# Hybrid decoder block on one core: half of the retention gates made by seven-product multiplication with the queries and keys, and 29 modulation rows summed in the values stage

## The chip, the core and the metric

The kernel runs on one core of a Trainium2 chip. TensorE (PE) multiplies, VectorE (DVE), ScalarE (ACT) and GpSimd (POOL) work element by element, SyncE (SP) issues most DMAs, and 16 DMA engines carry the data. The metric is the device time of one execution in microseconds (us). All numbers are float32; a matmul operand is split into a high part (rounded to the format `fp32r`) and a low remainder, and a product of two split operands is three matmuls: low x high, high x low, high x high.

## The reference, cut to what matters

A decoder block for 1024 tokens of width 1024: a conditioning vector gives six modulation vectors (shift, scale and gate, twice), a token mixer runs retention and dilated attention side by side, an MLP follows.

```python
mod = jax.nn.silu(c) @ w_ada[l] + b_ada[l]
sh1, sc1, g1, sh2, sc2, g2 = jnp.split(mod, 6, axis=-1)
h = modulate(rms_norm(x, norm1_g[l]), sh1, sc1)
proj = h @ w_in                       # rq, rk, rv, rg, attention's q, k, v, two gates
ro = retention(rq, rk, heads(rv))     # 4 heads, chunks of 128 tokens, a running state
ro = group_norm(ro)                   # per token and head, 512 values
ret_out = (jax.nn.silu(rg) * ro) @ w_ret_out
```

`rg` is 2048 wide: 512 columns for each of four heads, which the kernel treats as four blocks of 128 columns a head. `g1`, `sh2`, `sc2` and `g2`, 32 rows of 128 values together, are not needed until retention and attention are done.

## The kernel before, in words

**Layout.** `hh` and `hl` are the high and low part of the modulated input, transposed, eight tiles of 128 channels by 1024 tokens. Everything that multiplies `h` reads them.

**Order of the work.** `Steps` runs step after step; each engine executes its instructions in the order in which the code issues them. The stages that matter here come one after the other.

1. *Queries and keys* (`queries_keys`, line 1216 on, class `Blocks`). Products with weights are taken in pairs of 128 columns. A pair is a 2 x 2 block product done by seven block products (`ORDER`) in place of eight. Each of the seven is four steps of three matmuls of 512 columns. DVE and ACT make the weight sums and splits (`prep`), and take the results apart (`post`, `a_out`). `PAIRS` lists 20 pairs: eight with rotary, six queries and two keys of attention, four pairs of merge gates, which pass through Sigmoid and go to DRAM.
2. *Values* (`values`, line 1339). Ten block products (`VSEQ`), five for each pair of heads, each of four sub-steps of 12 matmuls, one for each 128 tokens. During sub-step `p` of product `i`, ACT and DVE finish the results of the sub-step before (`v_post`) and split the weights of product `i + 1` (`v_w` on ACT, `v_low` on DVE); at the head of a product SP reads the weights of product `i + 2` (`v_load`). Results of products 3, 4 (`i` = 2, 3) go through tiles `vo` of the pool `wraw` (tag `raw`, three buffers) to DRAM; those of products 8 and 9 take tiles of another pool, and those of 5 and 10 the tile that holds their sum. Some buffers of that pool serve as staging for every streamed weight.
3. *Chunks* (`chunk`, line 692). 4 heads x 8 chunks. A chunk updates the state (`kv` products, `state`, split to `stateh`/`statel`), makes the scores of the next chunk (`s_kt`: products `sT`, then `sm`, `smh`, `sml`, and the scaled keys `kh`, `kl`), its output `o`, the normalisation (`bn`, `ba`, `gr`, `onm`) and the transposes of the chunk before (`on_T`). Between these products PE works at a gate block: 4 of the 8 steps of a block in each chunk, six matmuls a step, in two portions. In the first four chunks of a head, `u_final` multiplies the head before by its gates (`on`, `srg`) and writes it out (`y`).
4. Attention, the output projections and the MLP follow; the change does not touch them.

**What sets the order around the change.** In a chunk step, `ahead(2)` prepares the loads of the next step: gate weights (ACT copy, DVE subtract, `split_w`) and modulation rows (`mod_prep`: one DVE multiply with the sum along the row, `accum_out`, and one small add). The step list gives a gate block to every second chunk and one of 32 modulation rows to nearly every chunk. Raw tiles come from `wraw`; the weights' halves from `whl` (three buffers each). PSUM has four single banks for `kv`, `sT`, `kT`, `o` and `oT` in turn and two double banks for gate blocks. A tile takes a buffer of its pool that no earlier tile still needs, and waits until there is one.

Of the kernel before, what the change touches and what calls it, by code (L numbers as in the profile page):

```python
# [17 lines left out]
P = 128  # L18
# [122 lines left out]
def block_kernel(ctx, tc, io, stop=None, dbg=None):  # L141
# [478 lines left out]
    def chunk_tiles():  # L620

        p = R["p"]
        R["j"] = p.tile([P, 2, 4, C], F32R, tag="j", bufs=2, name="j2")
        R["sm"] = p.tile([P, C], F32, tag="sm", bufs=1, name="sm00")
        for n in ("smh", "sml"):
            R[n] = p.tile([P, C], F32R, tag=n, bufs=2, name=n + "00")
        for n in ("kh", "kl"):
            R[n] = p.tile([P, 2, P], F32R, tag=n, bufs=1, name=n + "00")

    def s_kt(i):  # L630
# [49 lines left out]
    def u_final(h, es=range(4), queue=nc.sync):  # L680
        for e in es:
# [8 lines left out]
            queue.dma_start(y_d[h][:, 2 * (i % 2):2 * (i % 2) + 2, e // 2], t.rearrange("p (t x) -> p t x", t=2))  # L690

    def chunk(h, c, ahead, w=None):
        p = R["p"]
        g = NC * h + c
        if g + 3 < NG:
            fetch(g + 3)
        if c % 2 == 0:
            hd["rgw"] = w
            hd["rgp"] = ps_mm(f"rg{h}{c}")

        ks = {0: (5, 6, 6), 1: (6, 7, 8)}.get(g) or [4 * (c % 2) + i for i in (0, 2, 4)]
        if g == 0:
            proj_mm(hd["rgp"], hd["rgw"], range(2))
            s_kt(0)
            proj_mm(hd["rgp"], hd["rgw"], range(2, 5))
        vh, vl = hd["v", g][:, 0], hd["v", g][:, 1]
# [8 lines left out]
        if g == 0:  # L715
            s_kt(1)
        proj_mm(hd["rgp"], hd["rgw"], range(*ks[:2]))
        for i, kv in enumerate(kvs):
# [27 lines left out]
        if g > 0:  # L746
            on_T(*divmod(g - 1, NC))
        proj_mm(hd["rgp"], hd["rgw"], range(*ks[1:]))
        bn = p.tile([P, 6], F32, tag="bn", bufs=2, name=f"bn{h}{c}")
# [9 lines left out]
        hd["o", h, c] = on  # L759
        if c % 2 == 1:  # L760
            hd["srg", h, c // 2] = etile(f"srg{h}{c // 2}")
            nc.scalar.activation(hd["srg", h, c // 2], flat(hd["rgp"]), AF.Silu)
        if h > 0 and c < 4:
# [7 lines left out]
    aq_d = {(p, g, a): dram.tile([P, S], F32, name=f"aqd{p}{g}{a}") for p in range(2) for g in range(3) for a in range(2)}  # L771
    ak_d = {(p, a): dram.tile([P, S], F32, name=f"akd{p}{a}") for p in range(2) for a in range(2)}
    h12_d = [dram.tile([P, 2, 512], F32, name=f"h12d{m}") for m in range(4)]
    xn, wa = [], []
# [362 lines left out]
    k_pairs = [("k", 2, p) for p in range(2)]  # L1137
    PAIRS = [{"r": r_pairs, "a": a_pairs, "g": g_pairs, "k": k_pairs}[i].pop(0) for i in "rargrarkrargrarkgaga"]
    NA = len(PAIRS)
    OA = {}  # L1140

    def a_load(q, part):
        pair = PAIRS[q]
        src = io[{"g": "w_gate2", "a": "w_aq", "k": "w_ak2"}.get(pair[0]) or f"w_r{pair[1]}"]
# [22 lines left out]
    def a_out(q, n, x, y=None):  # L1167
# [9 lines left out]
        elif pair[0] in "ak" and pair[1] == 2:  # L1177
            o = OA[q][i].rearrange("p (r i) -> p r i", r=8)[:, :, 64 * t:64 * t + 64]
            view = lambda z: z.rearrange("p (i r) -> p r i", r=8)
        f = AF.Sigmoid if pair[0] == "g" else AF.Copy  # L1180
        if y is None:
            nc.scalar.activation(o, view(x), f)
        else:
            (nc.vector.tensor_add if n == "12" else nc.vector.tensor_sub)(o, view(x), view(y))
            if pair[0] == "g":
                nc.scalar.activation(o, o, f)
        if n in ("12", "21"):
            if pair[0] == "g":
                dst = gate_d[GATES[2 * pair[1] + i]]
            elif pair[0] == "a":  # L1190
                dst = aq_d[pair[2], pair[1], i]
            elif pair[0] == "k":
                dst = ak_d[pair[2], i]
            else:
                return
# [137 lines left out]
    def v_base_load(hp):  # L1333

        for j in range(2):
            V["m", hp, j] = t = x4(f"vm{hp}{j}")
            nc.sync.dma_start(t.rearrange("p (a b) -> p a b", a=2), m11_d[hp][:, 2 * j:2 * j + 2])

    def values(ahead):
        last = len(VSEQ) - 1  # L1340
        for i, (hp, n) in enumerate(VSEQ):
            if i + 2 <= last:
                v_load(i + 2)
            for p in range(4):
# [14 lines left out]
                if p == 2 and i < last:  # L1359
                    v_low(i + 1, 1)  # L1360

                if i == last - 2 and p == 2:
                    fetch(0)
# [13 lines left out]
        for g in (1, 2):  # L1377
# [9 lines left out]

    later_mods = [G1 + k for k in range(NK)] + [SH2 + k for k in range(NK)] + \
                 [SC2 + k for k in range(NK)] + [G2 + k for k in range(NK)]
# [1432 lines left out]
def pack(x, c, w_ada, b_ada, norm1_g, w_in, rel_bias, ret_gn_g, ret_gn_b,  # L2822
# [16 lines left out]
        "w_rv": _vblocks(w[:, 2048:4096]),  # L2839
        "w_rg": _cols(w[:, 4096:6144]),  # L2840
        "w_aq": _pairs(att[:, :, 0].reshape(1024, 1536)),
# [32 lines left out]
```

## Time and profile before

| | |
|---|---|
| median of three runs | 2176.75 us (2176.67 to 2182.43) |
| the profiled execution | 2179.79 us, span 2178.0 us, granted clock 0.997 |
| PE | 99% of the span, 10060 matmuls |
| DVE / ACT / POOL | 69% / 43% / 8% |
| HBM | 322.03 MB read, 158.23 MB written, 221 GB/s over the span |

In the profile, a row of a timeline holds the start, the time occupied, the engine, the line in kernel.py, the operation, the tiles written and read with their shape, and in brackets the idle time before it and what ended it. "L1285 DVE ... vwl<-vwl,vwh" is line 1285 on VectorE, which writes `vwl` from `vwl` and `vwh`. A row of a table of stretches has, for a stretch of the span, each engine's busy time and number of instructions. A row of waits names who waited, for whom, the sum, how often, and the longest. A row of DMA issues ends with the median time from issue to landing.

### The profile page before, as it was taken

How to read it: one execution, taken by the hardware profiler on the slowest of the kernel's cores; microseconds unless marked ns; L12 is line 12 of the kernel's file. 1: busy time of each engine (PE TensorE's matmuls, PEld its weight loads, DVE VectorE, ACT ScalarE, POOL GpSimd, SP SyncE). 2: the span in 40 equal slices, each digit the busy share in tenths (PEclk: the TensorE clock that was granted, in tenths of full speed). 3: DMA queues.
4: the chain of work that ended last, by engine and by line, in shares of the span. 5: the costliest groups of instructions: out<-in, count | busy, mean ns of one | idle time of the engine just before them, and what ended most of it. 6: DMA issues, size and time to landing. Idle time of an engine off the chain costs nothing. (4 is left out here: it accounts for less than half of the span.)

```text
span 2178.0 us, 27354 instructions
## 1 busy us (share of the span) xinstructions
PE 2151.7 (99%) x10060; PEld 1789.6 (82%) x10060; DVE 1512.8 (69%) x2361; ACT 947.4 (43%) x1741; POOL 167.2 (8%) x199
## 2 busy tenths in 40 slices
PE   8999999999999999999999999999999999999998
PEld 6888888888887888888888888888778888888887
DVE  5885777776346787785657644777876665877855
ACT  5553322323343354455657625434454445533413
POOL 0001111100002121211110000001000000000003
PEclk9999999999999999999999999999999999999999
DMA  9759998833568455546777275653244435645322
GB/s 383 282 212 311 270 334 255 235 110 116 184 240 295 160 203 182 173 168 196 205 192 209 98 260 196 222 188 136 66 179 153 153 136 195 248 138 174 109 87 78
DMA packets 161522, 420.98 MB, mean 193 GB/s; under 512 B 27877, under 2 KB 55788, under 8 KB 158316
## 3 DMA queue, kind: packets, MB, share of 16 engines
q1 hardware_dynamic: 149112, 370.70, 47.7%
q0 software_dynamic: 9584, 48.24, 9.8%
q8 instruction: 79, 1.29, 0.2%
q10 hardware_dynamic: 2692, 0.30, 0.1%
q14 instruction: 55, 0.45, 0.1%
HBM read 322.03 MB, written 158.23 MB: 221 GB/s over the span
## 5 line engine op out<-in xcount | busy, mean ns | idle before, releaser
L207 PE MATMUL qap<-hh,qaw 128*128 128x512 f32 x240 | 93.4, 389 | 0.0
L209 PE MATMUL qap<-hl,qaw 128*128 128x512 f32 x240 | 93.4, 389 | 0.0
L211 PE MATMUL qap<-hh,qaw 128*128 128x512 f32 x240 | 93.4, 389 | 0.0
L617 POOL TENSOR_TENSOR j<-qk,j 128x512 fp32r<-128x512 f32 x32 | 43.2, 1351 | 457.5 <-ACT j L616 457.5
L2193 POOL TENSOR_TENSOR accnf<-accnf,sqnf 128x256 f32<-128x256 f32 (+1 forms) x18 | 16.6, 921 | 609.6 <-ACT sqnf L2189 609.6
L2297 ACT ACTIVATE a<-a 128x512 f32<-128x512 f32 x48 | 30.3, 631 | 73.3 <-DVE a L2296 73.3
L2505 ACT CAST w2h<-w2s 128x512 fp32r<-128x512 f32 x36 | 22.4, 621 | 78.7 <-DVE w2s L2543 71.8
L264 DVE TENSOR_TENSOR fw<-w1r,fw 128x512 fp32r<-128x512 f32 x48 | 32.9, 688 | 33.5 <-ACT fw L254 33.5
L209 PEld LDWEIGHTS qap<-hl,qaw 128*128 128x128 f32 x240 | 45.0, 188 | 9.4
L211 PEld LDWEIGHTS qap<-hh,qaw 128*128 128x128 f32 x240 | 45.0, 188 | 9.3
L207 PEld LDWEIGHTS qap<-hh,qaw 128*128 128x128 f32 x240 | 45.0, 188 | 9.3
L652 ACT COPY sm<-sT 128x128 f32<-128x128 f32 x32 | 8.5, 265 | 98.9 <-PE sT L640 91.4
L2028 DVE TENSOR_TENSOR rwl<-rwl,rwh 128x1024 fp32r<-128x1024 f32 x25 | 30.2, 1221 | 29.0 <-ACT rwh L2058 29.0
L207 PE MATMUL fp<-h2h,fw 128*128 128x512 f32 x128 | 50.0, 391 | 0.0
L211 PE MATMUL fp<-h2h,fw 128*128 128x512 f32 x128 | 49.8, 389 | 0.0
L209 PE MATMUL fp<-h2l,fw 128*128 128x512 f32 x128 | 49.8, 389 | 0.0
L207 PE MATMUL roa<-rh,rwl 128*128 128x512 f32 x128 | 49.8, 389 | 0.0
L209 PE MATMUL roa<-rl,rwh 128*128 128x512 f32 x128 | 49.8, 389 | 0.0
L211 PE MATMUL roa<-rh,rwh 128*128 128x512 f32 x128 | 49.8, 389 | 0.0
L1561 ACT ACTIVATE P<-P,ng 128x128 f32<-128x128 f32 (+1 forms) x96 | 41.9, 438 | 17.5 <-DVE ng L1553 17.5
L264 DVE TENSOR_TENSOR qaw<-wa,qaw 128x512 fp32r<-128x512 f32 x60 | 40.0, 686 | 8.8 <-ACT qaw L254 8.8
L292 DVE TENSOR_TENSOR qat<-qat,qap 128x512 f32<-128x512 f32 x20 | 13.7, 687 | 46.4 <-PE qap L211 46.4
(3094 smaller groups left out, 7241.4 us busy)
## 6 DMA issues: line engine op xcount, KB each, us to landing
v<-vd SPq DMA_DIRECT2D x32, 512.0 KB, 4.3
raw<-in_w_ada_dram SPq DMA_DIRECT2D x32, 512.0 KB, 5.0
w1r<-in_w_ff_dram SPq DMA_DIRECT2D x32, 512.0 KB, 4.6
yt<-y POOLq DMA_DIRECT2D x24, 512.0 KB, 7.4
xsd<-as SPq DMA_DIRECT2D x24, 512.0 KB, 2.9
w2r<-in_w_ff2s_dram SPq DMA_DIRECT2D x24, 512.0 KB, 6.7
em<-in_w_ada_dram SPq DMA_DIRECT2D x16, 512.0 KB, 10.2
wrvs<-in_w_rv_dram POOLq DMA_DIRECT2D x16, 512.0 KB, 9.6
```

Of the source, the lines that this page charges most:

```text
L207: nc.tensor.matmul(o, wl, xh, start=first, stop=False, skip_group_check=skip)
L209: nc.tensor.matmul(o, wh, xl, start=False, stop=False, skip_group_check=skip)
L211: nc.tensor.matmul(o, wh, xh, start=False, stop=last, skip_group_check=skip)
L264: nc.vector.tensor_sub(t[:, 512:], src, fv(t[:, :512]))
L292: nc.vector.tensor_sub(u, u, b)
L617: nc.gpsimd.tensor_sub(t[:, 1], src, fv(t[:, 0]))
L652: nc.scalar.copy(sm, ps[:, :C])
L1561: nc.scalar.activation(v, v, AF.Exp, bias=ng[:, blk:blk + 1], accum_out=st[:, g, blk, 2 + a:3 + a])
L2028: nc.vector.tensor_sub(lo, fv(lo), fv(hi))
L2193: (nc.vector if f == 7 else nc.gpsimd).tensor_add(G["acc", key], G["acc", key], sq)
L2297: nc.scalar.activation(o, o, AF.Relu)
L2505: nc.scalar.copy(hi, src)
```

## The change

1. The 16 gate blocks are parted: of each head, blocks 0 and 1 stay in the chunks; blocks 2 and 3 become a pair of the queries-and-keys stage (`"s"`, after all other pairs), pass through Silu there and go to DRAM (`srg_d`). The fifth and the seventh chunk of a head read them back. The weights are rearranged on the host's side accordingly.
2. In the chunks, a table `RG` says how many gate steps each does: 6 in the first of all, then 2, and 1 in the last chunk of a head (64 in all). A block may start in the middle of a head; `rg_mm` takes the next weights and PSUM tile when one is done, `rg_out` applies Silu.
3. 29 of the 32 later modulation rows are read and summed in the values stage, at places listed in `MODS`: six each in products 1 and 2, five each in 5, 6 and 7, two in 8. A call loads row `i` and sums row `i - 2`. The three left stay in the chunks, one in the fifth of each head but the first.
4. `chunk_tiles` allocates the tile `j` last and not first.

```diff
+    RG = [[2] * (NC - 1) + [1] for _ in range(H)]
+    RG[0][0] = 6
+    def rg_mm(n):
+        for _ in range(n):
+            if hd.get("rgk", NK) == NK:
+                hd["rgk"], hd["rgw"], hd["rgp"] = 0, hd["rgws"].pop(0), ps_mm("rg")
+            proj_mm(hd["rgp"], hd["rgw"], [hd["rgk"]])
+            hd["rgk"] += 1
+            if hd["rgk"] == NK:
+                hd["rgs"] = hd["rgp"]
+    def rg_out(h, c):
+        if "rgs" in hd:
+            i = hd["rgi"] = hd.get("rgi", -1) + 1
+            t = hd["srg", i // 2, i % 2] = etile(f"srg{i // 2}{i % 2}")
+            nc.scalar.activation(t, flat(hd.pop("rgs")), AF.Silu)
+        if c in (4, 6):
+            e = c // 2
+            hd["srg", h, e] = etile(f"srg{h}{e}")
+            nc.sync.dma_start(hd["srg", h, e], srg_d[h, e - 2])
...
     def chunk(h, c, ahead, w=None):
...
-        proj_mm(hd["rgp"], hd["rgw"], range(*ks[:2]))
+        rg_mm(1 if g == 0 else RG[h][c] - 1)
...
-        proj_mm(hd["rgp"], hd["rgw"], range(*ks[1:]))
+        rg_mm(0 if g == 0 else 1)
...
-        if c % 2 == 1:
-            hd["srg", h, c // 2] = etile(f"srg{h}{c // 2}")
-            nc.scalar.activation(hd["srg", h, c // 2], flat(hd["rgp"]), AF.Silu)
+        rg_out(h, c)
...
-    PAIRS = [{"r": r_pairs, "a": a_pairs, "g": g_pairs, "k": k_pairs}[i].pop(0) for i in "rargrarkrargrarkgaga"]
+    s_pairs = [("s", i) for i in range(H)]
+    PAIRS = [{"r": r_pairs, "a": a_pairs, "g": g_pairs, "k": k_pairs, "s": s_pairs}[i].pop(0)
+             for i in "rargrarkrargrarkgagassss"]
...
-        f = AF.Sigmoid if pair[0] == "g" else AF.Copy
+        f = {"g": AF.Sigmoid, "s": AF.Silu}.get(pair[0], AF.Copy)
...
+            elif pair[0] == "s":
+                dst = srg_d[pair[1], i]
...
+    MODS = [(i, p) for i in (0, 1, 4, 5, 6, 7) for p in range(4) if i < 7 or p < 2
+            for _ in range(2 if i < 2 and p % 2 or p == 3 else 1)]
+    NV = len(MODS)
+    def values_mod(i):
+        if i < NV:
+            t = V["mod", i] = wraw.tile([P, 1024], F32, tag="raw", name=f"vmod{i}")
+            nc.sync.dma_start(t, io["w_ada"][G1 + i])
+        if i > 1:
+            t, m = V.pop(("mod", i - 2)), G1 + i - 2
+            nc.vector.scalar_tensor_tensor(t, t, 1.0, cb, op0=ALU.mult, op1=ALU.mult, accum_out=mods[:, m:m + 1])
+        if i == NV + 1:
+            m = mods[:, G1:G1 + NV]
+            nc.vector.tensor_add(m, m, vec[:, VC_BADA + G1:VC_BADA + G1 + NV])
...
     def values(ahead):
...
                 if p == 2 and i < last:
                     v_low(i + 1, 1)
+                for j, at_ in enumerate(MODS):
+                    if at_ == (i, p):
+                        values_mod(j)
+                if (i, p) == MODS[-1]:
+                    values_mod(NV)
+                    values_mod(NV + 1)
...
-                      ([wsplit(io["w_rg"][4 * h + c // 2])] if c % 2 == 0 else []) +
-                      [mod_load(later_mods[8 * h + i]) for i in ({0: (0, 1), 1: ()}.get(8 * h + c, (c,)))],
+                      ([wsplit(io["w_rg"][RGW.index(NC * h + c)])] if NC * h + c in RGW else []) +
+                      ([later_mod()] if h > 0 and c == 4 else []),
```

More of the change, by code (lines that the diff above doesn't have):

```diff
@@ L622, in chunk_tiles @@
         p = R["p"]
-        R["j"] = p.tile([P, 2, 4, C], F32R, tag="j", bufs=2, name="j2")
         R["sm"] = p.tile([P, C], F32, tag="sm", bufs=1, name="sm00")
@@ L628, in chunk_tiles @@
             R[n] = p.tile([P, 2, P], F32R, tag=n, bufs=1, name=n + "00")
+        R["j"] = p.tile([P, 2, 4, C], F32R, tag="j", bufs=2, name="j2")
     def s_kt(i):
@@ L696, in chunk @@
             fetch(g + 3)
[L697 to L701, printed above, removed]
+        if w is not None:
+            hd.setdefault("rgws", []).append(w)
         if g == 0:
-            proj_mm(hd["rgp"], hd["rgw"], range(2))
+            rg_mm(2)
             s_kt(0)
-            proj_mm(hd["rgp"], hd["rgw"], range(2, 5))
+            rg_mm(3)
         vh, vl = hd["v", g][:, 0], hd["v", g][:, 1]
@@ L772, in block_kernel @@
     ak_d = {(p, a): dram.tile([P, S], F32, name=f"akd{p}{a}") for p in range(2) for a in range(2)}
+    srg_d = {(h, i): dram.tile([P, S], F32, name=f"srgd{h}{i}") for h in range(H) for i in range(2)}
     h12_d = [dram.tile([P, 2, 512], F32, name=f"h12d{m}") for m in range(4)]
@@ L1143, in a_load @@
         pair = PAIRS[q]
-        src = io[{"g": "w_gate2", "a": "w_aq", "k": "w_ak2"}.get(pair[0]) or f"w_r{pair[1]}"]
+        src = io[{"g": "w_gate2", "a": "w_aq", "k": "w_ak2", "s": "w_rg2"}.get(pair[0]) or f"w_r{pair[1]}"]
         i = 2 * pair[1] + pair[2] if pair[0] == "a" else pair[-1]
@@ L1184, in a_out @@
             (nc.vector.tensor_add if n == "12" else nc.vector.tensor_sub)(o, view(x), view(y))
-            if pair[0] == "g":
+            if pair[0] in "gs":
                 nc.scalar.activation(o, o, f)
@@ L1386, in block_kernel, with later_mod @@
     steps.add(queries_keys, manual=True)
-    later_mods = [G1 + k for k in range(NK)] + [SH2 + k for k in range(NK)] + \
-                 [SC2 + k for k in range(NK)] + [G2 + k for k in range(NK)]
+    RGW, n = [], 0
+    for g in range(NG):
+        RGW += [g] * (n < 8 * len(RGW) + 1 <= n + RG[g // NC][g % NC])
+        n += RG[g // NC][g % NC]
+    late_mods = iter(range(G1 + NV, 48))
+    def later_mod():
+        return mod_load(next(late_mods))
     for h in range(H):
@@ L2839, in pack @@
         "w_rv": _vblocks(w[:, 2048:4096]),
-        "w_rg": _cols(w[:, 4096:6144]),
+        "w_rg": _cols(w[:, 4096:6144].reshape(1024, 4, 4, P)[:, :, :2].reshape(1024, 1024)),
+        "w_rg2": _pairs(w[:, 4096:6144].reshape(1024, 4, 4, P)[:, :, 2:].reshape(1024, 1024)),
         "w_aq": _pairs(att[:, :, 0].reshape(1024, 1536)),
```

## The prediction, made before the changed kernel ran

> **What bounds the kernel now.** I read the page first, then the table of stretches, then the timelines of TensorE (PE) and VectorE (DVE).
>
> ```profile
> span 2178.0 us, 27354 instructions
> PE 2151.7 (99%) x10060; PEld 1789.6 (82%) x10060; DVE 1512.8 (69%) x2361; ACT 947.4 (43%) x1741; POOL 167.2 (8%) x199
> ```
>
> PE is occupied in 2151.7 of 2178.0 us, so for the span a product saved is worth its own pitch, as long as what feeds PE keeps up. That has to be read stage by stage. The next rows are the queries-and-keys stage, its last pair but one, the values stage, the first head's chunks from its second on, then the next two heads. The columns are length, then busy time and count of PE, PEld, DVE, ACT and POOL, granted clock, DMA share, GB/s.
>
> ```profile
> 180.50:561.30 380.80, 380.80 (x1681) 315.32 (x1681) 268.71 (x414) 110.02 (x192) 36.23 (x50) 1.00 0.72 225
> 523.20:542.20 19.00, 19.00 (x85) 15.73 (x85) 9.91 (x15) 5.76 (x10) 0.00 (x0) 1.00 0.14 55
> 561.30:671.10 109.80, 109.02 (x482) 89.93 (x481) 52.95 (x65) 46.54 (x68) 7.13 (x10) 1.00 0.70 249
> 690.00:754.00 64.00, 63.20 (x310) 52.34 (x309) 51.49 (x111) 27.98 (x74) 13.23 (x14) 1.00 0.52 171
> 754.00:831.60 77.60, 77.60 (x380) 64.52 (x379) 62.98 (x132) 37.23 (x93) 15.13 (x16) 1.00 0.57 190
> 831.60:909.10 77.50, 77.50 (x380) 64.46 (x379) 62.91 (x132) 37.21 (x93) 15.13 (x16) 1.00 0.57 191
> ```
>
> PE is full in all of them, but DVE is at 63 of 77.5 us in a head and only at 53 of 109.8 in the values. The pitch of a 512-wide matmul is not its 389 ns but the distance of starts; here are six pairs of gate matmuls, then the same score product one chunk later:
>
> ```profile
> 960.41 0.62 PE L207 MATMUL rg<-hh,raw_7772l 128*128 128x512 f32 x2
> ...
> 963.13 0.28 PE L638 MATMUL sT<-j 128*128 128x256 f32 x1
> ...
> 973.13 0.28 PE L638 MATMUL sT<-j 128*128 128x256 f32 x1
> ```
>
> Twelve matmuls take 963.13 - 960.41 = 2.72 us, 0.2267 each; a chunk takes 10.00, of which its 24 gate matmuls are 5.44. Now one chunk on DVE, from one normalised output (onm) to the next, with a split and a modulation row in it:
>
> ```profile
> 785.29 0.81 DVE L758 TENSOR_SCALAR onm<-o,ba,gr 128x512 f32<-128x512 f32 x1
> 786.02 1.22 DVE L689 TENSOR_TENSOR on<-on,srg 128x1024 f32<-128x1024 f32 x1
> 787.15 1.28 DVE L725 SCALAR_TENSOR_TENSOR state<-state,kv 128x512 f32<-128x512 f32 x2
> 788.35 1.22 DVE L198 TENSOR_TENSOR raw_6146l<-raw,raw_6146h 128x1024 fp32r<-128x1024 f32 x1
> 789.49 1.22 DVE L464 SCALAR_TENSOR_TENSOR raw<-raw,cb 128x1024 f32<-128x1024 f32 x1
> ...
> 790.82 0.28 DVE L653 TENSOR_TENSOR sm<-sm,sT 128x128 f32<-128x128 f32 x1
> 791.14 0.29 DVE L654 TENSOR_TENSOR sm<-sm,decay 128x128 f32<-128x128 f32 x1
> 791.79 0.29 DVE L656 TENSOR_TENSOR sml<-sm,smh 128x128 fp32r<-128x128 f32 x1 [0.36 <-ACT smh L655]
> 792.17 0.48 DVE L666 SCALAR_TENSOR_TENSOR kl<-kT,ct,kh 128x256 fp32r<-128x256 f32 x1
> 792.68 1.30 DVE L743 TENSOR_TENSOR statel<-state,stateh 128x512 fp32r<-128x512 f32 x2
> 793.89 0.69 DVE L752 BATCH_NORM_STATS2 bn<-o 128x6 f32<-128x512 f32 x1
> ...
> 795.71 0.16 DVE L756 TENSOR_TENSOR gr<-gr,ct 128x1 f32<-128x1 f32 x1 [0.66 <-POOL gr L755]
> 795.98 0.81 DVE L758 TENSOR_SCALAR onm<-o,ba,gr 128x512 f32<-128x512 f32 x1
> ```
>
> The chain is 10.69 us and has no gap but two short hops, 0.36 for ACT and 0.66 for POOL, which belong to it. In these four chunks of a head DVE is as full as PE. Without the split (789.49 - 788.35 = 1.14) and the row (790.82 - 789.49 = 1.33) it is 8.22; without the gating multiply of the head before (787.15 - 786.02 = 1.13) too, 7.09.
>
> **Queries and keys.** Four pairs are added. Each is seven products of four steps of three matmuls, 84 x 0.2267 = 19.04 us, as the 20 pairs there show (380.8 / 20). A gate pair in the second row has DVE at 9.9 and ACT at 5.8 of 19.0, so operand sums, splits, Silu in place of Sigmoid, 1 MB in and 1 MB out all lie under PE. **+76.2**. If that cover failed, the Silu pass would cost at most its own 1 us a pair.
>
> **Chunks.** 64 of 128 steps of six matmuls go: 87.1 us of PE (64 x 6 x 0.2267). A full chunk then needs 10.00 - 2.72 = 7.28 of PE. DVE loses 29 of 32 rows and 8 of 16 splits, but not its 8.22 chain. The score product of the next chunk cannot start before onm frees its PSUM bank, and the scores' split waits for it, so the two engines cannot drift apart by more than a chunk. I take the later of the two for each chunk of a later head:
>
> - four with the gating multiply: 8.2 each, 32.8
> - the first (state chain whole, its kv products only just ahead; estimate): 7.5
> - a middle one, PE 7.28: 7.3, and the one row that is left: 1.3
> - the one without a key split: PE, 7.1
> - the last, with no kv, no state update, one gate step: DVE 8.22 - 1.13 - 1.20 - 1.21 = 4.7, with the wait for its own output 5.3 (estimate)
> - two splits in a head: 1.14 in a gated chunk, about 0.9 in another
>
> That is 63.3 against 77.5, a gain of 14.2; three heads, 42.6. In the first head the gate multiply is absent and its first two chunks keep their eight gate steps: 8.2 + 3 x 7.3 + 8.2 + 7.1 + 5.3 = 50.7 against 64.0, a gain of 13.3. Together **-56**, not -87. The 31 us between are PE standing for DVE. The split gate loads (eight writes earlier, eight reads by SP in the fifth and seventh chunk of a head) fall where SP has only its fetches, three chunks ahead; I cost them at nothing. The other place of tile j is worth between -1 and +1, taken as nothing.
>
> **Values.** 29 rows are read and summed here: DVE 29 x 1.33 = 38.6 on top of 53 of 109.8 us. Room there is, but DVE works in order, and a row that has not landed holds the weight splits behind it, which PE needs for its next product (48 matmuls, 10.88). The raw pool has three buffers. Rows:
>
> ```profile
> raw<-in_w_ada_dram SPq DMA_DIRECT2D x32, 512.0 KB, 5.0
> ```
> ```profile
> 590.51 0.69 DVE L1324 TENSOR_TENSOR vo<-vr,vo 128x512 fp32r<-128x512 f32 x1 [0.69 <-ACT vo L1323]
> ...
> 600.91 1.22 DVE L1283 TENSOR_TENSOR vwl<-vwl,vwh 128x1024 fp32r<-128x1024 f32 x1
> ```
> ```profile
> ACT vo L1317 <- DMA vd<-vo: 6.1, 2, 3.2
> ```
> ```profile
> vd<-vo SPq DMA_DIRECT2D x1, 512.0 KB, 2.6
> ```
> ```profile
> vd<-vo SPq DMA_DIRECT2D x1, 512.0 KB, 8.6
> ```
>
> The last two are result writes, one issued in 588 to 590 and one in 598 to 599.5: 2.6 us to land when alone, 8.6 when several are under way. With three buffers a row costs (5.0 + 1.2 + 0.3) / 3 = 2.2 us (0.3 for the issue, estimate), so the twelve rows in products 1 and 2 keep DVE until about 590, where the first result of product 3 was at 586.
>
> What decides is the list of places: a row is loaded two calls before its sum, and after the twelfth there is no call until product 5. Rows 11 and 12 hold two raw buffers through products 3 and 4, whose eight results (vo) are written to the same pool, until now through three buffers, with ACT already waiting for two of them (third row group). With one, each result waits for the write before: 0.69 for ACT's cast, 0.69 for the low part, 0.2 for the issue (estimate), 2.6 to land, 4.2 us, where PE makes one in 2.72. The second half of product 5's weights (row 600.91) stands behind the sixth result: 590.7 + 5 x 4.2 + 1.4 + 1.2 = 614.3. PE wants it at 604.9 + 1.4 = 606.3: 8 to 9 us. In product 5 DVE then has four results of 2.1, two splits of 1.2 and five rows of 1.3, 17 of 10.9: 5.5 more. Product 8 has three results, two splits and four sums, 14 of 10.9, after rows that land late: 5 more. **+20**, between nothing (were every landing covered) and 60 (8 x (1.6 + 8.6) for the results, less 21.8); I take the unloaded landing, since the writes now come one by one.
>
> Queued on SP behind the held row loads are the weights of two products on; they were issued up to 25 us early, and there is slack. The rows' bytes: 27.4 MB in the stage now, some 14 more, 41 MB.
>
> ```profile
> 659.40:671.10 11.70, 10.92 (x50) 8.70 (x48) 8.07 (x15) 2.46 (x4) 2.76 (x6) 1.00 1.09 390
> DMA packets 8788, 27.40 MB, mean 249 GB/s; under 512 B 876, under 2 KB 1900, under 8 KB 8782
> ```
>
> The first row has 390 GB/s over 11.7 us; at that rate 41 MB are 105 us, under the stage's 110, so bytes are no term of the sum. The Trainium skill, DMA: Bandwidth & Descriptors (section Specifications), gives about 358 GB/s as HBM's limit for a core; by it the stage would be 115 us, 5 more. The trace went above that figure, and the measurement decides.
>
> **Sum.** +76.2 - 56 + 20 = +40. The profiled execution took 2179.8 (span 2178.0 and 1.8 around it), 3 above the median 2176.75. So 2219.8 by the one, **2216** by the other, which I forecast.
>
> **Rivals.**
> - *DVE keeps up, the time falls.* If the 8.2 chain could overlap its neighbour, so that PE alone set the chunks, and the rows were hidden: 76.2 - 87.1 = -10.9, 2166. For it: PE shows no gap in a head now. Against it: the chain is serial on one engine. It decides where the later heads' chains fall from 63 to under 56.6 us (77.5 less (76.2 - 13.3) / 3).
> - *The values hide all.* Landings are short and PE's slack of 9 to 14 us for each split is enough: 2176.75 + 20 = 2197. For it: DVE has 57 free us there.
> - *Landings are long.* At 5.2 us, between the two rows, a result takes 6.8, eight take 54 and not 34: 20 more, 2236.
> - *The clock falls.* The chunks' start, which had short waits, shows what a pause can do:
>
> ```profile
> 671.10:690.00 18.90, 16.11 (x67) 12.84 (x68) 5.84 (x15) 5.90 (x13) 1.85 (x2) 0.91 0.85 310
> ```
>
> A clock of 0.91 over 18.9 us is 1.7 us lost. Three pauses of 5 us and more in the values would cost some 5 us: 2221. The Trainium skill, TensorE: Matmul & The Clock Gate (What's actually happening), says that an idle window of about 3.4 us halves the clock until one busy window has passed; the row has a lower clock after pauses, so it agrees in direction.
>
> **Chances.** Forecast 0.45, its own range 2205 to 2227; values hidden 0.2; long landings 0.2; clock 0.08; faster 0.05; 0.02 within 0.3% of before (6.5 us, about what a measurement can tell). Slower 0.93, faster 0.05. The range that leaves out 2 in 10 goes from the hidden values to the long landings with some room: 2192 to 2242.
>
> **What would show it.** In the chunks of later heads, onm every 8.2 us in four chunks, DVE without gaps and PE waiting before sT, released by onm. In the values, ACT waiting for vd<-vo at nearly each result of products 3 and 4, and PE waiting for vwl at product 5. Queries and keys 24 x 19.04 = 457 us. It would be wrong if onm came every 7.3 us in gated chunks, or if the values stage kept its 110 us.

## The result, and the profile after

The changed kernel takes 2232.3 us (median of five runs, 2230.97 to 2233.52), the kernel before 2176.67 beside it: a ratio of 1.0251, interval 1.0240 to 1.0263, 55.6 us slower. The sign was forecast. The time lies inside the range, 16 us above the forecast of 2216.

First the head of the changed kernel's page; the profiled execution took 2233.52 us.

```profile
span 2231.5 us, 27383 instructions
PE 2162.0 (97%) x10012; PEld 1789.5 (80%) x10012; DVE 1540.6 (69%) x2389; ACT 960.1 (43%) x1773; POOL 167.7 (8%) x199
```

PE has 48 matmuls fewer and is busy 10 us longer. So fewer products did not give less PE time: some matmuls got slower, and PE stood idle for 69.5 us instead of 26. The table of stretches of the changed kernel says where. Its rows are queries and keys, values, the start of the chunks up to the first normalised output (`onm`), and the four heads (the first from its first `onm` to its last, each later one from the last `onm` of the head before to its own); the columns are those of the table in the prediction.

```profile
180.40:637.60 457.20, 457.20 (x2019) 378.57 (x2018) 309.56 (x477) 138.57 (x240) 36.22 (x50) 1.00 0.67 206
637.60:788.50 150.90, 121.02 (x481) 95.30 (x480) 84.73 (x118) 46.81 (x70) 7.15 (x10) 0.92 0.79 279
788.50:803.40 14.90, 14.42 (x69) 11.47 (x69) 6.55 (x17) 5.91 (x13) 1.85 (x2) 1.00 1.02 363
803.40:852.80 49.40, 47.96 (x240) 39.30 (x239) 39.58 (x89) 23.61 (x70) 13.19 (x14) 1.00 0.50 153
852.80:916.40 63.60, 58.78 (x277) 47.62 (x276) 51.30 (x108) 33.46 (x89) 15.02 (x16) 0.95 0.53 173
916.40:979.40 63.00, 57.30 (x278) 46.67 (x277) 51.21 (x108) 33.23 (x89) 15.07 (x16) 0.97 0.53 176
979.40:1042.20 62.80, 56.98 (x273) 46.24 (x273) 50.10 (x104) 31.69 (x85) 12.41 (x14) 0.97 0.37 123
```

Together with the same stretches of the kernel before, its fourth head too (76.85 in the same view), they give this account:

| stretch | before | after | difference | forecast |
|---|---|---|---|---|
| queries and keys | 380.8 | 457.2 | +76.4 | +76.2 |
| values | 109.8 | 150.9 | **+41.1** | +20 |
| start of the chunks | 18.9 | 14.9 | -4.0 | none |
| four heads, as above | 295.9 | 238.8 | -57.1 | -56 |
| all that follows | 1192.1 | 1189.3 | -2.8 | none |

Together +53.6, where the spans differ by 53.5. One term is wrong, the values, by 21 us; the two gains that were not forecast return 7 of it. The rows of the heads also show that PE now stands idle for 4.8 to 5.8 us in each later head, where it had no idle time before.

**The heads.** The timeline of DVE in the changed kernel, its `onm` and one modulation row (two ungated chunks of the first head, then chunks of the second head, in which the head before is multiplied by its gates):

```profile
818.68 0.81 DVE L779 TENSOR_SCALAR onm<-o,ba,gr 128x512 f32<-128x512 f32 x1
825.87 0.81 DVE L779 TENSOR_SCALAR onm<-o,ba,gr 128x512 f32<-128x512 f32 x1
...
870.05 0.81 DVE L779 TENSOR_SCALAR onm<-o,ba,gr 128x512 f32<-128x512 f32 x1
878.25 0.81 DVE L779 TENSOR_SCALAR onm<-o,ba,gr 128x512 f32<-128x512 f32 x1
...
881.33 1.22 DVE L464 SCALAR_TENSOR_TENSOR raw<-raw,cb 128x1024 f32<-128x1024 f32 x1
...
887.83 0.81 DVE L779 TENSOR_SCALAR onm<-o,ba,gr 128x512 f32<-128x512 f32 x1
```

An ungated chunk takes 7.19 us, a gated one 8.20, and a gated one with the modulation row that is left 9.58; the one before these, gated and with a weight split, takes 9.35 (860.70 to 870.05). The row has its place in the fifth chunk, but it is summed earlier, while the gated chunks run. And PE's waits over the three later heads (who waited for whom, sum, times, longest):

```profile
PE o L207 <- DVE state L746: 11.7, 12, 1.3
PE kT L645 <- DVE onm L779: 3.0, 7, 0.5
PE sT L638 <- POOL j L617: 1.6, 2, 1.2
```

In the twelve gated chunks PE waits for DVE's state update.

**The values.** PE's waits in that stage of the changed kernel:

```profile
PE va L209 <- DVE vwl L1309: 17.1, 6, 7.6
PE vc L209 <- DVE vwl L1307: 9.9, 4, 3.8
PE va L209 <- DVE vwlTrue L1309: 2.9, 1, 2.9
```

They sum to 29.9 us, which is all of PE's idle time (150.90 - 121.02), and every one is for a weight split. By products the eleven pauses are 2.9 us in product 2, 3.6 in 3, 2.4 in 4, 7.1 in 5, 2.8 in 6, 0.3 in 7, 2.3 in 8 and 8.5 in 9. The longest can be read off DVE's timeline:

```profile
755.10 1.22 DVE L1309 SCALAR_TENSOR_TENSOR vwl<-vwl,vwh 128x1024 fp32r<-128x1024 f32 x1
756.23 1.22 DVE L1374 SCALAR_TENSOR_TENSOR vmod<-vmod,cb 128x1024 f32<-128x1024 f32 x1
...
758.43 1.23 DVE L1374 SCALAR_TENSOR_TENSOR vmod<-vmod,cb 128x1024 f32<-128x1024 f32 x1 [0.97 <-DMA vmod<-in_w_ada_dram]
...
760.99 1.23 DVE L1374 SCALAR_TENSOR_TENSOR vmod<-vmod,cb 128x1024 f32<-128x1024 f32 x1 [1.33 <-DMA vmod<-in_w_ada_dram]
...
764.33 1.22 DVE L1309 SCALAR_TENSOR_TENSOR vwl<-vwl,vwh 128x1024 fp32r<-128x1024 f32 x1
```

Between the two halves of one split stand three row sums, for two of which DVE waits until their bytes have landed, and a result. 9.2 us pass from one half to the other. PE's timeline at the end of that pause:

```profile
765.61 0.80 PE L209 MATMUL va<-vwl,hh 128*128 128x512 f32 x1 [7.58 <-DVE vwl L1309]
766.20 0.63 PE L211 MATMUL va<-vwh,hh 128*128 128x512 f32 x1
766.63 0.63 PE L207 MATMUL va<-vwh,hl 128*128 128x512 f32 x1
```

Starts are now 0.427 us apart and no longer 0.227, and so until 770.9. That is the second part of the loss: the stage's 481 matmuls at 0.2267 are 109.0 us, and PE was busy for 121.0, with a granted clock of 0.92. Of these 12.0 us, 10.0 are lost behind the five pauses that slow matmuls follow; the rest is mostly some 0.3 us at each other restart. 109.0 + 29.9 + 12.0 = 150.9.

Last, the results of products 3 and 4. ACT's timeline, the first two of eight and the last four, and then two rows of ACT's waits in the stage:

```profile
672.25 0.62 ACT L1347 CAST vo<-vr 128x512 fp32r<-128x512 f32 x1 [7.98 <-DVE vr L1346]
680.58 0.62 ACT L1347 CAST vo<-vr 128x512 fp32r<-128x512 f32 x1 [6.74 <-DMA vd<-vo]
...
693.78 0.60 ACT L1341 ACTIVATE vo<-va 128x512 fp32r<-128x512 f32 x1 [3.12 <-DMA vd<-vo]
700.46 0.60 ACT L1341 ACTIVATE vo<-va 128x512 fp32r<-128x512 f32 x1 [5.14 <-DMA vd<-vo]
704.51 0.60 ACT L1341 ACTIVATE vo<-va 128x512 fp32r<-128x512 f32 x1 [3.45 <-DMA vd<-vo]
708.91 0.60 ACT L1341 ACTIVATE vo<-va 128x512 fp32r<-128x512 f32 x1 [3.80 <-DMA vd<-vo]
```
```profile
ACT vo L1341 <- DMA vd<-vo: 15.5, 4, 5.1
ACT vo L1347 <- DMA vd<-vo: 14.0, 3, 6.7
```

Seven of the eight results wait for the write before them, as forecast; from first to last 36.7 us pass, 5.24 each. Five of the seven distances are 4.1 to 4.7 us, and two are longer, 8.3 and 6.7.

### The profile page after: what moved, and what is told of

Same layout as the page of the kernel before. It is cut to its first block, busy times and chain, and to the rows that moved or that the text cites. A ratio compares the mean times of both kernels' runs of the same rounds, so it can differ in the third digit from the quotient of the medians.

```text
span 2231.5 us, 27383 instructions
## 1 busy us (share of the span) xinstructions
PE 2162.0 (97%) x10012; PEld 1789.5 (80%) x10012; DVE 1540.6 (69%) x2389; ACT 960.1 (43%) x1773; POOL 167.7 (8%) x199
## 3 DMA queue, kind: packets, MB, share of 16 engines
q8 instruction: 79, 1.29, 0.2%
## 5 line engine op out<-in xcount | busy, mean ns | idle before, releaser
L207 PE MATMUL qap<-hh,qaw 128*128 128x512 f32 x288 | 112.0, 389 | 0.0
L209 PE MATMUL qap<-hl,qaw 128*128 128x512 f32 x288 | 112.0, 389 | 0.0
L211 PE MATMUL qap<-hh,qaw 128*128 128x512 f32 x288 | 112.0, 389 | 0.0
L207 PEld LDWEIGHTS qap<-hh,qaw 128*128 128x128 f32 x288 | 54.1, 188 | 11.2
L211 PEld LDWEIGHTS qap<-hh,qaw 128*128 128x128 f32 x288 | 54.1, 188 | 11.2
L209 PEld LDWEIGHTS qap<-hl,qaw 128*128 128x128 f32 x288 | 54.1, 188 | 11.2
L264 DVE TENSOR_TENSOR qaw<-wa,qaw 128x512 fp32r<-128x512 f32 x72 | 48.1, 686 | 11.6 <-ACT qaw L254 11.6
L1374 DVE SCALAR_TENSOR_TENSOR vmod<-vmod,cb 128x1024 f32<-128x1024 f32 x29 | 35.2, 1223 | 19.7 <-DMA vmod<-in_w_ada_dram 19.5
```

Of the source, the lines that this page charges most:

```text
L207: nc.tensor.matmul(o, wl, xh, start=first, stop=False, skip_group_check=skip)
L209: nc.tensor.matmul(o, wh, xl, start=False, stop=False, skip_group_check=skip)
L211: nc.tensor.matmul(o, wh, xh, start=False, stop=last, skip_group_check=skip)
L264: nc.vector.tensor_sub(t[:, 512:], src, fv(t[:, :512]))
L1374: nc.vector.scalar_tensor_tensor(t, t, 1.0, cb, op0=ALU.mult, op1=ALU.mult, accum_out=mods[:, m:m + 1])
```

## The experiments

The theory after the result: the gates alone cost a little, because DVE's chain sets the chunks; the rest is the rows' in the values, through three mechanisms (two rows held in the pool of three; rows ahead of splits in DVE's order; bytes). The rivals: DVE's time as such, or the bytes as such. Differences below are between medians.

### 1. No rows at all

```diff
-                for j, at_ in enumerate(MODS):
-                    if at_ == (i, p):
-                        values_mod(j)
                 if (i, p) == MODS[-1]:
-                    values_mod(NV)
-                    values_mod(NV + 1)
+                    nc.vector.memset(mods[:, G1:G1 + NV], 0.5)
```

> The 29 modulation rows are neither read nor summed (their 29 values are set to 0.5, so the output is another one); the gates stay as in the changed kernel. Theory: all the added time of the values stage (150.9 us against 109.8) comes from the rows, so the stage goes back to 110 and the kernel to 2232.3 - 41 = 2191 us, still 14 above before, because the chunks stay bound by DVE (onm every 8.2 us). Rival, the gates moved are what stalls the values (writes of the last Silu pair, DMA at their start): 2220 or more.

2192.44 us, 1.0069 of before (1.0054 to 1.0084). Its table of stretches, the values and the second head:

```profile
638.10:747.00 108.90, 108.90 (x481) 90.02 (x481) 50.53 (x60) 47.48 (x70) 7.12 (x10) 1.00 0.69 247
...
811.50:875.10 63.60, 58.84 (x277) 47.83 (x277) 51.43 (x108) 33.33 (x89) 15.11 (x16) 0.95 0.53 174
```

The values stage is full again, and the four heads together are within 0.5 us of the changed kernel's. So the rows cost 39.9 us (2232.3 - 2192.4), nothing of it through the chunks; the gates in product form, with those rows nowhere, cost 15, where PE's count alone would give -10.9. That part of the forecast (2191) stands.

### 2. Both held rows summed before product 3

```diff
...
+        if i == 11:
+            mod_sum(10)
+            mod_sum(11)
```

`mod_sum` sums a row once; the later call finds it done.

> One edit: rows 11 and 12 are summed where they are loaded, at the end of product 2, so that no raw buffer is held through products 3 and 4. Theory (held buffers are the larger half of the stall): the eight results come at PE's pace again, 21.8 us in place of 36.7 for their seven gaps and one more, and most of the lowered clock of that stretch (0.82 over 19 us, 3.5 us) goes too: 2232.3 - 18 = 2214, between 2208 and 2220; the stalls of products 1, 2, 5 to 8 stay. Rival, the rows' landings in DVE's order are the whole cost: 2228 or more, because two more sums stand ahead of product 3's splits.

2221.18 us, 1.0205 (1.0190 to 1.0220): 11.1 less than with the change, not 18, and just above the range. The values stage in the table of stretches, then all of PE's longer waits in it, then ACT's `vo` (the first, and of the last four three):

```profile
637.90:773.20 135.30, 115.78 (x482) 92.14 (x481) 84.11 (x118) 46.72 (x70) 8.03 (x10) 0.95 0.84 308
```
```profile
PE va L209 <- DVE vwl L1309: 15.5, 8, 7.7
PE va L209 <- DVE vwlTrue L1309: 3.3, 1, 3.3
```
```profile
678.05 0.62 ACT L1347 CAST vo<-vr 128x512 fp32r<-128x512 f32 x1 [12.86 <-DVE vr L1346]
...
689.20 0.59 ACT L1341 ACTIVATE vo<-va 128x512 fp32r<-128x512 f32 x1
694.23 0.60 ACT L1341 ACTIVATE vo<-va 128x512 fp32r<-128x512 f32 x1 [4.45 <-DMA vd<-vo]
698.17 0.60 ACT L1341 ACTIVATE vo<-va 128x512 fp32r<-128x512 f32 x1 [3.34 <-DMA vd<-vo]
```

The eight results now take 20.1 us and not 36.7, and no pause of PE in product 5 is left (7.1 us with the change): the mechanism is the held buffers. It is worth less than it looks, for one thing because the first result comes 5.8 us later, since the two sums brought forward, each of which waits for its bytes, stand ahead of it on DVE. The pauses in products 2, 3, 4 and 9 stay, nearly all with the same releaser. In this profile the values stage is 15.6 us shorter and the heads are 1.4 longer, so 11.1 is the smaller of two readings of what the held buffers cost.

### 3. Rows loaded, not summed

The sums are left out; the 29 values are set to 0.5.

```diff
-            t = V["mod", i] = wraw.tile([P, 1024], F32, tag="raw", name=f"vmod{i}")
+            t = wraw.tile([P, 1024], F32, tag="raw", name=f"vmod{i}")
             nc.sync.dma_start(t, io["w_ada"][G1 + i])
-        if i > 1:
-            t, m = V.pop(("mod", i - 2)), G1 + i - 2
-            nc.vector.scalar_tensor_tensor(t, t, 1.0, cb, ...)
...
```

> The 29 rows are read into their raw buffers at the same places but never summed (values set to 0.5, another output). A buffer is free as soon as its row has landed. Theory: bytes are not the limit (41 MB at the 390 GB/s seen are 105 us), SP only waits for landings: 2191 to 2200. Rival, HBM traffic is the limit (the Trainium skill's 358 GB/s would make the stage 115 us or more, and results land late): 2205 to 2232.

2200.75 us, 1.0108 of before: 8.3 more than without rows, between the two forecasts. The values stage in its table of stretches:

```profile
637.00:752.50 115.50, 111.53 (x481) 90.85 (x481) 49.15 (x60) 46.82 (x70) 7.81 (x10) 0.99 0.97 352
```

PE is idle for 4.0 us. The DMA engines are 0.97 busy. So loading has a price of its own, though it is far from the whole. Whether the bytes make it, or the buffers and the place in SP's order that the loads take, this run does not part.

### 4. Rows summed, not loaded

Here `cb` is multiplied with itself 29 times and no row is read; each sum takes a raw tile only while it runs.

```diff
-            t = V["mod", i] = wraw.tile([P, 1024], F32, tag="raw", name=f"vmod{i}")
-            nc.sync.dma_start(t, io["w_ada"][G1 + i])
         if i > 1:
-            t, m = V.pop(("mod", i - 2)), G1 + i - 2
-            nc.vector.scalar_tensor_tensor(t, t, 1.0, cb, ...)
+            t, m = wraw.tile([P, 1024], F32, tag="raw", name=f"vmod{i}"), G1 + i - 2
+            nc.vector.scalar_tensor_tensor(t, cb, 1.0, cb, ...)
```

> The 29 sums run at the same places on a resident tile in place of a loaded row (another output); nothing is loaded and no raw buffer is held. Theory: DVE has room (53 of 110 us busy, 38.6 added), what costs is waiting for landings and for buffers; only product 8, where four sums meet three results and two splits, is late by some 3 us: 2191 to 2198. Rival, DVE's own time is what costs: 2215 or more.

2195.34 us, 1.0082: 2.9 more than without rows, with four times from 2192.0 to 2198.9, so hardly clear of noise. Its values stage:

```profile
637.00:748.00 111.00, 109.96 (x482) 89.69 (x481) 82.32 (x118) 46.51 (x70) 8.03 (x10) 1.00 0.65 234
```

DVE is as busy as with the whole change (82 us against 85), and PE stands for 1 us. Both rivals fall: 32 us of DVE's time (82.3 against 50.5) cost 3, the loads 8. The greater part of the 39.9 comes where sum and load depend on each other. With the held buffers (11.1), 8.3 and 2.9, 17.6 remain for waiting sums ahead of splits; that is a difference, not a measurement.

### 5. Gates alone, rows in the chunks as before

```diff
-    MODS = [(i, p) for i in (0, 1, 4, 5, 6, 7) for p in range(4) ...]
+    MODS = []
...
-                      ([later_mod()] if h > 0 and c == 4 else []),
+                      [later_mod() for _ in ({0: (0, 1), 1: ()}.get(8 * h + c, (c,)))],
```

> Only the gates' part of the change: the 32 rows stay in the chunks as before, the values stage is that of before. Theory (DVE's serial chain sets the chunks): 29 rows of 1.33 us come back on DVE, 38.6, less about 6 of slack in the short last chunks and those without gating: 2192.4 (the kernel without rows) + 33 = 2225, between 2217 and 2231. Rival, PE or a latency sets the chunks: rows hide, 2192 to 2200.

2223.76 us, 1.0214. The heads are 58.4, 71.7, 71.4 and 68.1 us, together 30.8 above the changed kernel's. In the chunks, once PE no longer hides DVE, 29 rows cost 31.3 us over none at all (2223.8 - 2192.4), about 1.1 each.

Against the kernel before, the gates alone cost 46.5 us, not the little of the theory above: the 15 of experiment 1 hold only where the rows are nowhere. Moving the 29 rows to the values as the change does made this 8.5 us worse.

### 6. Rows alone, gates as before

The opposite: before's gates, and the 29 rows with `MODS` and `values_mod` in its values stage.

```diff
...
+                for j, at_ in enumerate(MODS):
+                    if at_ == (i, p):
+                        values_mod(j)
...
-                      [mod_load(later_mods[8 * h + i]) for i in ({0: (0, 1), 1: ()}.get(8 * h + c, (c,)))],
+                      ([mod_load(44 + h)] if h > 0 and c == 4 else []),
```

> Only the rows' part: 29 rows in the values stage, all gates in the chunks as before. Theory: the values stage gets its 40 us as in the changed kernel; the chunks are full on PE (10.0 us each, 77.0 of 77.5 in a head), so freeing DVE there gives back only 0.5 a head, 1 to 3 in the first head and some 4 at the chunks' start: 2177 + 40 - 7 = 2210, between 2204 and 2217. Rival, the rows were what held the chunks before: 15 to 25 back, 2192 to 2202.

2214.69 us, 1.0168, 37.4 above before. Values and second head:

```profile
561.30:711.50 150.20, 122.81 (x483) 96.55 (x481) 83.80 (x119) 46.16 (x68) 8.14 (x10) 0.90 0.79 281
...
789.60:866.70 77.10, 77.10 (x379) 64.44 (x378) 54.28 (x110) 37.48 (x93) 15.16 (x16) 1.00 0.44 144
```

The loss in the values is the same without any change of the gates. And DVE, freed of 8.7 us in a head, shortens it by 0.4: there PE is the bound, and what DVE saves is worth next to nothing.

### 7. The gating multiply left out

In the chunks of heads 2 to 4 the head before is not multiplied by its gates.

```diff
-            nc.vector.tensor_mul(t, t, hd["srg", h, e])
+            if mul:
+                nc.vector.tensor_mul(t, t, hd["srg", h, e])
...
-            u_final(h - 1, (c,))
+            u_final(h - 1, (c,), mul=False)
```

> The changed kernel without the gating multiply on DVE in the first four chunks of heads 2 to 4 (three of four heads go ungated, another output). Theory (the 8.2 chain is DVE's): those chunks fall to PE's 7.28 plus some coupling, 0.9 each of 12, and 1.1 where a split stands too: 2232.3 - 12 = 2220, between 2217 and 2223. Rival, the chain's length is latency between engines (PSUM banks, score product, hops): the multiply lies in a gap, 2230 to 2233.

2215.89 us, 1.0178: 16.4 less than with the change. The heads are 49.4, 58.3, 58.5 and 56.8. DVE's timeline, two `onm` in the second head's early chunks:

```profile
867.27 0.81 DVE L780 TENSOR_SCALAR onm<-o,ba,gr 128x512 f32<-128x512 f32 x1
874.34 0.81 DVE L780 TENSOR_SCALAR onm<-o,ba,gr 128x512 f32<-128x512 f32 x1
```

7.07 us, where a gated chunk has 8.20: the multiply's whole 1.13. PE's products are the same in both kernels, so DVE's chain, not PE, sets the gated chunks. The twelve multiplies are 13.6 us of DVE; 16.4 went, a little more than the range of the expectation allowed. Two of the twelve chunks had been longer to begin with: in the fourth gated chunk of heads 2 and 4, 8.72 and 8.98 us in the changed kernel, PE ran slow matmuls (starts 0.43 us apart) after pauses of 0.5 and 1.3 us, and the granted clock of its three later heads, 0.95 to 0.97, is 1.00 here.

### 8. Half as many gates as pairs

One block of a head as a pair and three in the chunks, six rows in the values behind both splits, 26 in the chunks.

```diff
-    RG = [[2] * (NC - 1) + [1] for _ in range(H)]
-    RG[0][0] = 6
+    RG = [[3] * NC for _ in range(H)]
+    RG[0] = [6, 2, 3, 3, 3, 3, 2, 2]
...
-    s_pairs = [("s", i) for i in range(H)]
+    s_pairs = [("s", i) for i in range(H // 2)]
...
+    MODS = {(1, 0): ([0, 1, 2], []), (1, 2): ([], [0]), (1, 3): ([], [1, 2]),
+            (6, 0): ([3, 4, 5], []), (6, 2): ([], [3]), (6, 3): ([], [4, 5])}
```

> One gate block of four per head by seven products (two pairs, blocks 3 of two heads each); three steps of gates in a chunk, so PE 8.64 against DVE 8.2. Rows: none in the gated chunks; 26 in the others (two in the first and in the last chunks of a head), six in the values, in products 2 and 7 where DVE and DMA are emptiest, three read at a product's head and summed behind its splits, none held over. Theory: queries +38.1, chunks 32 steps less, -43.5 on PE, of which some 3 to 5 are lost where a split or a row makes DVE late: 2176.7 - 2 = 2175, between 2171 and 2180. Rival, in which the chunks cannot follow PE below 10 us at all: 2195 or more.

2187.02 us, 1.0045 (1.0032 to 1.0057), a miss: slower, not even. The values are 109.5 us, as hoped; the heads are 60.9, 71.1, 69.7 and 67.7. DVE's timeline in a fourth chunk:

```profile
824.42 0.81 DVE L778 TENSOR_SCALAR onm<-o,ba,gr 128x512 f32<-128x512 f32 x1
825.15 1.22 DVE L689 TENSOR_TENSOR on<-on,srg 128x1024 f32<-128x1024 f32 x1
...
827.48 1.22 DVE L198 TENSOR_TENSOR raw_6199l<-raw,raw_6199h 128x1024 fp32r<-128x1024 f32 x1
828.62 1.22 DVE L464 SCALAR_TENSOR_TENSOR raw<-raw,cb 128x1024 f32<-128x1024 f32 x1
...
835.09 0.81 DVE L778 TENSOR_SCALAR onm<-o,ba,gr 128x512 f32<-128x512 f32 x1
```

Gate multiply, split and row fall in one chunk: 10.67 us. The rows were given to the last four chunks so as to miss the gated four, but a load is prepared, and summed, one chunk ahead of its place.

### 9. Eighteen rows, each behind both splits, none held

Eleven rows are left at 0.5 and cost nothing. Of the others, three are loaded at the head of products 1, 2, 5, 6, 7 and 8, and summed in that product's third and fourth sub-step, after `v_low`.

```diff
+    for n, i in enumerate((0, 1, 4, 5, 6, 7)):
+        j = 3 * n
+        MODS[i, 0], MODS[i, 2], MODS[i, 3] = ([j, j + 1, j + 2], []), ([], [j]), ([], [j + 1, j + 2])
```

> The changed kernel with 18 of the 29 rows (the other 11 values set to 0.5, another output), three in each of the same six products: read together at the product's head, summed behind both of its splits, none held over. Theory (what costs beyond bytes and DVE time is a row that has not landed standing ahead of a split, and the buffers held): 2192.4 without rows, plus 18/29 of the 8 for the loads and 3 for the sums that the runs gave, 7: 2199, between 2194 and 2205. Rival, rows cost in proportion wherever they stand (40 us for 29): 2192.4 + 25 = 2217.

2193.77 us, 1.0075: 1.3 us above no rows, where the same eighteen at the change's price (39.9 / 29 each) would cost 24.8. The values stage:

```profile
637.00:746.00 109.00, 109.00 (x483) 90.24 (x482) 71.54 (x96) 46.69 (x70) 8.03 (x10) 1.00 0.90 329
```

No idle time and a full clock, though DVE still waits there for rows in seven places (6.6 us together): a wait behind the splits costs PE nothing. This is the nearest to a direct measurement of the 17.6, on eighteen rows and not on 29. The time lies just under the expected range, whose 7 us for loads and sums did not come.

### 10 and 11. Versions meant to beat before

Number 10 is number 8 with twelve rows in the values, behind the splits, and those in the chunks placed one chunk later. Number 11 is the kernel before, its gates untouched, with eighteen rows behind the splits and fourteen in chunks without a gating multiply.

```diff
-                      [later_mod() for _ in range(([2, 1, 1, 1, 1, 1, 2, 2] if h == 0 else [0, 0, 0, 0, 1, 1, 1, 2])[c])],
+                      [later_mod() for _ in range(([2, 0, 1, 1, 1, 1, 1, 1] if h == 0 else [2, 0, 0, 0, 0, 0, 1, 1])[c])],
```

> The one-block kernel, in which loads are prepared one chunk ahead, so that rows of the fifth chunk were summed in the fourth, gated one (onm distances of 10.67). Now no row falls in a gated chunk: 12 rows in the values (products 1, 2, 6, 7), two with a head's first chunk, one each with the seventh and eighth. Theory: the heads go from 71.1, 69.7 and 67.7 towards PE's 66.6 plus what two splits cost: 68 each, 5 less, 2182, between 2178 and 2185, if the six further rows in the values hide too. Rival, the gated chunks with a split alone hold PE: 2186 to 2188.

2182.14 us, 1.0022 (1.0013 to 1.0031). Heads 60.9, 70.2, 68.6 and 65.6: 4.9 us better than number 8, and still 5.3 above before. Its gated chunks with a split still take 9.34 us, where PE needs 8.64 by the count of experiment 8.

```diff
-                      [mod_load(later_mods[8 * h + i]) for i in ({0: (0, 1), 1: ()}.get(8 * h + c, (c,)))],
+                      [mod_load(next(late_mods)) for _ in range(([2, 0, 1, 1, 1, 1, 0, 0] if h == 0 else [h < 3, 0, 0, 0, 0, 0, 1, 1])[c])],
```

> All 16 gate blocks in the chunks as before; of the 32 rows, 18 in the values, three to a product behind its splits, the other 14 in chunks without the gating multiply. Theory: the rows in the values cost 0 to 1.5, and the chunks give back what the rows-only kernel got there, 0.9 in the first head and 0.4 in each other: 2176.9 - 1 = 2176, between 2173 and 2178, at the limit of what can be told from no change. Rival, in which rows held the chunks before: 2165 or less.

2179.29 us, 1.0012 (1.0003 to 1.0021): 2.4 us above before, by an interval that just leaves out no change, and 1.3 above the expected range. Moving rows out of chunks in which PE is the bound gains nothing, as number 6 said. The kernel before stays the fastest of all that ran.

## Why the prediction was right in part, and where it was wrong

- **Queries and keys, +76.2: right** (76.4). 24 pairs at 19.05, PE full, DVE, ACT and DMA under it.
- **Chunks, -56: right** (-57.1; later heads 63.6, 63.0 and 62.8 for 63.3, the first 49.4 for 50.7). The reason holds too: a plain gated chunk goes at 8.20 and not at PE's 7.28, and experiment 7 took the multiply away and got 1.1 to 1.9 us back in each gated chunk, 1.13 in a plain one. Within a later head errors offset each other: the first chunk took 7.9 for 7.5, the last 4.7 (3.9 in the fourth head) for 5.3, the row fell in a gated chunk and not in a middle one, and two gated chunks with slow matmuls took 8.7 and 9.0 for 8.2. One sign was wrong: PE was to wait ahead of `sT`, released by `onm`. It waits ahead of `o`, for the state (11.7 of 16.3 us), so the same chain binds at another of its links.
- **Values, +20: wrong; this is the step that failed.** Its mechanism was right. Rows 11 and 12 hold two of three buffers, the results wait one by one, PE waits for `vwl` in product 5, and also in products 6 and 9, because DVE fell behind in the products before them. For these three the forecast had 8 to 9, 5.5 and 5 us, together about 19; measured are 7.1, 2.8 and 8.5, 18.4. That the sums agree is in part luck, since the single terms are off by 1.4 to 3.5 us, not all to one side (and the working's own 8.4 + 2.4 + 6.5 less 10.9 for product 5 is 6.4, not 5.5). What the sum lacked are two terms.
  - *Rows ahead of splits in the other products:* 2.9, 3.6, 2.4, 0.3 and 2.3 us in products 2, 3, 4, 7 and 8, 11.5 in all. The working said that a row that has not landed holds the splits behind it, and let DVE run till 590 on that account, but took PE's slack for large enough everywhere outside products 5, 6 and 9. It was not: `MODS` puts sums ahead of a split and between its halves, and experiment 9, which puts fewer of them, all behind, has no pause at all.
  - *The clock:* 10.0 us behind the pauses that slow matmuls follow, 12.0 with the other restarts. It stood as a rival, with a chance of 0.08 and 5 us from three pauses, and should have been a term of the sum, since the pauses were in the sum. Of eleven pauses, four were 3.37 us or longer (3.37, 3.63, 3.75, 7.58); after each, starts came 0.427 us apart for 2.9 to 5.7 us, 1.6 to 2.7 us lost a time. The Trainium skill, TensorE: Matmul & The Clock Gate (What's actually happening), has the clock halved after an idle window of about 3.4 us until a busy one of that length has passed. The trace agrees for these four, and for six of 0.19 to 2.85 us after which 0.3 to 0.7 us were lost; but a pause of 2.59 us was followed by eight slow matmuls, 1.9 us, as well, and in the three later heads, where no pause is longer than 1.32 us, the clock was halved four times. So here shorter pauses were enough.
- **"Bytes are no term of the sum": wrong by a little.** Loading alone costs 8.3 us (experiment 3), though by bytes or by buffers is not shown. The 390 GB/s of the trace held for 11.7 us, and over a whole stage the runs reach 352. The Trainium skill, DMA: Bandwidth & Descriptors (Specifications), gives HBM's limit for a core as about 358 GB/s, from which the prediction estimated 115 us for the stage; experiment 3 has 115.5. That does not show the limit to be the cause: in the table the rate goes up to 363 GB/s in the chunks' start, and 329 in experiment 9 cost nothing.
- **4.2 us a result: low.** It was 5.24 on average. Five of the seven distances, 4.1 to 4.7 us, agree with it; the two long ones, 8.3 and 6.7, have a write that SP issued 3 to 4 us behind other loads (two of weights, two of partial sums, 512 KB each), which suggests that the writes then did not have the DMA engines to themselves, but no run tried it. That cost less than it might: PE was late in products 2 to 4 as well, and asked later.
- **The chunks' start, -4.0, was not forecast.** The 2.8 us of idle time there became 0.5, and the clock rose from 0.91 to 1.00. The kept traces narrow it: from the first gate product to the first `onm` it takes 15.6 us in experiment 5, with the rows back in the chunks, and 15.0 in experiment 6, with the gates back, so either part alone brings most of it. By what mechanism was not tried, nor were the 2.8 us gained behind the chunks.

What stays open is how the 17.6 us divide between late rows and the DVE time of the sums in front of the splits. Number 4 speaks for the former: the same sums in the same places, never late, cost 2.9. A deeper pool of raw tiles was not tried, nor were all 29 rows behind the splits.

## What to carry to other kernels

Taking products from a loop in which the next engine is nearly as full gains only down to that engine's serial chain: here 57 of 87 us, while the price elsewhere was paid in full. Work for a free engine goes behind the instructions that its critical neighbour waits for, not between them; there even a wait for its own bytes cost PE nothing, and 18 rows cost 1.3 us where in proportion to the change they would have cost some 25. A list of places that looks ahead by two keeps two buffers wherever it pauses, so it is to be drained before another user of the pool comes; and where a forecast has pauses of several microseconds for PE, the slow matmuls after them are a term, here 10 us beside 30.

## What the runs showed of the hardware that was not expected

In these traces the granted clock of PE is either 1.00 or 0.50. Two rows of the table of stretches of the changed kernel show it, the first behind the pause of 2.59 us in the values, the second in the second head, behind pauses of 0.48 and 1.29 us:

```profile
720.20:723.40 3.20, 3.20 (x9) 2.50 (x8) 2.52 (x5) 0.62 (x1) 0.00 (x0) 0.50 0.62 238
863.60:866.80 3.20, 3.20 (x8) 2.44 (x8) 2.69 (x7) 1.26 (x4) 0.00 (x0) 0.50 1.04 316
```

Such a stretch lasts about 3.41 us, behind the pause of 7.58 us three times that, and the stretches start at whole multiples of 3.41 us from one another: those at 668.8, 696.1, 703.0, 720.0, 761.0 and 863.4 us (by the granted clock of stretches of 0.2 us) are 8, 2, 5, 12 and 30 times 3.41 us apart. The pause of 2.85 us had no such stretch and that of 2.59 us had one, so a pause's length alone does not decide; whether its place on this raster does was not tried. Behind the pause of 7.58 us the slow matmuls came at once; behind that of 3.63 us the first four distances of starts were 0.23 to 0.35 us and the next seven 0.43, so a short stretch of a timeline right after a pause can look healthy.

The DMA engines carried 329 GB/s at 0.90 busy without any loss for PE, and 352 at 0.97 with one of 8.3 us in the kernel's time: the step from free to dear was a narrow one in these two runs, which differ in the number of rows, in their places and in whether they are summed.
